# Passage from the output projection to the FFN up projection: first up operand and weights in the last output block, y a block ahead, written order

## Chip, cores and metric

One NeuronCore of a Trainium2 chip. The metric is the device time of one execution in microseconds, given as the median of several runs.

## What is computed

One layer of a hybrid decoder trunk on x (2048 x 1024, float32): a mixer of three head groups (mLSTM, forgetting attention, spatial gating), whose concatenated outputs y are projected back, and a convolutional FFN. The part that matters here:

```python
y = jnp.concatenate([y_attn, y_mlstm, y_sgu], axis=-1)        # (2048, 1024)
x = x + gt1 * (y @ w_out)                                     # output projection, residual
h = rms_norm(x, g_ffn) * (1.0 + sc2) + sh2
z = causal_depthwise_conv(h @ w_up, w_conv, b_conv)           # w_up: 1024 x 5632, width 3
a, gv = jnp.split(z, 2, axis=-1)
x = x + gt2 * ((silu(a) * gv) @ w_down)                       # w_down: 2816 x 1024
```

## The kernel before

It runs as stages: input projection with mLSTM and gating, attention, output projection, up with conv and gate, down. A float32 product is made of three matmuls of split operands (`mm3`, lines 54 to 56: high x high, high x low, low x high). A split is a copy of the high half on ScalarE (ACT) and a subtraction for the low half on VectorE (DVE).

**Output projection** (lines 1237 to 1264). The 2048 rows are four blocks of 512 in the order `TBS` = (2, 3, 0, 1). A block has eight parts `mm(i, nb)`: 128 rows i by a 512-column half nb of w_out, each 8 slices k of the contraction times three matmuls into one of four PSUM banks `wps`. Blocks 0 and 3 (counted in the order of the run) go by halves, the others by rows. `load_split` loads a piece of y or w_out into a buffer `ld` (for the four attention slices two pieces, added), and splits it into `yhl0`/`yhl1` (y; a block and a half fit) or `wo0`/`wo1`. `load_w(1)`, the second half of w_out, is called in block 0; `load_y` for a block at the block's start. `evict` multiplies a bank by the gate, adds x, lets ACT square and sum it, and stores x to DRAM; `stats` and `scale` make the RMS norm (the power is taken on GpSimd, POOL). `turns` transposes a finished block on TensorE (PE), 8 slices of four 128 x 128 transposes into four PSUM tiles `tps`, and ACT moves each slice with scale and shift into `hT`, the operand of up. The blocks of the second half of the sequence (H = 1) are combined and sent to DRAM (`put_d`, through `todo`).

**Up** (lines 1288 to 1404, loop from 1637). The product runs as seven steps p of a Strassen-like scheme for each group g of 128 + 128 columns and each half H. A step is 12 matmuls. Step p uses operand `OF[p]` of the sequence side: B11 and B21 are the first block's halves of hT as they are, B12 and B22 the second's, and T1 = B12 - B11, T2 = B22 - T1, T3 = B22 - B12, T4 = B21 - T2. `b_first` makes one, as 4 split tiles. `prep` makes the weight side (for p 5 and 6 the sums S1, S2 of weight blocks, lines 1326 and 1327), split into `wsp`; `mm` multiplies; `post` reads the PSUM bank on ACT or DVE (s1 for p = 1, u2 for p = 6, line 1366, za for p = 2, zg for p = 7 and 4); p = 2, 7 and 3 add into a bank that p = 1, 6 and 5 began and that s1, u2 and zg read in between. The first two groups run interleaved, step by step: 14 opening steps 0 to 13. `prep` runs three steps ahead (`AHEAD`).

What sets the order: a scheduler lays out each engine's queue from a simulated run, taking the instruction that is ready and stands first in the code. Memory is a stack from each side (`pool.open`, `pool.close`): a tile waits for the earlier tiles at its place. In the kernel before, `w` and B11 lie over buffers of `wo_r2`: `w` mostly over `yhl1`, B11 over `wo1`.

Of the kernel before, what the change touches and what calls it, by code (L numbers as in the profile page):

```python
# [33 lines left out]
def trunk(  # L34
# [257 lines left out]
    def wout_open_right():  # L292
        pool.open("wo_r", "right", ("yhl0", 2048, 16), ("ld", 2048, 3), ("wo0", 2048, 16))
# [845 lines left out]
    def load_y(n, tb):  # L1139

        tag = lambda k: "yhl%d" % ((n * 8 + k) % 12 >= 8)
        part = lambda d, k: d[k * P : (k + 1) * P, tb * TB : (tb + 1) * TB]
        return [load_split(part(yt_d, k), tag(k), V, part(y2_d, k) if k < 4 else None) for k in range(KT)]
# [6 lines left out]
    def put(n, q, t, by_dram=False):  # L1150

        if n == "T2":
            src = t[:, 1, :].bitcast(F32) if by_dram else pool.tile([P, 512], F32, name="t2")
            V.tensor_tensor(src, h_part("B22", q), h_part("T1", q), op=ALU.subtract)
            V.tensor_tensor(h_part("T4", q), h_part("B21", q), src, op=ALU.subtract)
        else:
            src = h_part(n, q)
            if n == "T1":
                V.tensor_tensor(src, h_part("B12", q), h_part("B11", q), op=ALU.subtract)
            elif n == "T3":  # L1160
                V.tensor_tensor(src, h_part("B22", q), h_part("B12", q), op=ALU.subtract)
        A.copy(t[:, 0, :], src)
        V.tensor_tensor(t[:, 1, :], src, t[:, 0, :].bitcast(F32), op=ALU.subtract)

    def put_d(n, q):
        t = pool.tile([P, 2, 512], F32R, name="hl", tag="hl")
        put(n, q, t, True)
        dma(hc_d[COMBO.index(n), q], t.bitcast(F32))

    class Block:  # L1170
        def __init__(self, n, tb):
            self.n, self.tb, self.H, self.half = n, tb, tb // 2, tb % 2
            self.x, self.st, self.ps, self.xn = {}, {}, {}, {}

        def start(self):
            self.y = load_y(self.n, self.tb)
# [45 lines left out]
        def turns(self):  # L1222
            if self.half == 0:
                for k in range(KT):
                    self.turn(k)
                if self.H == 1:
                    for q in range(4):
                        todo.append(lambda q=q: (put_d("B11", q), put_d("B21", q)))
            else:
                for q in range(4):  # L1230
                    self.turn(q)
                    self.turn(4 + q)
                    if self.H == 1:
# [6 lines left out]
    for n, tb in enumerate(TBS):  # L1240
        blk = Block(n, tb)
        blk.start()
        parts = by_nb if n in (0, 3) else by_i
        for j, (i, nb) in enumerate(parts):
            if (n, j) == (0, 4):
                load_w(1)
            blk.mm(i, nb)
            if n == 3 and j > 4:
                continue
# [5 lines left out]
            if j == 1 and before:  # L1255
                before.turns()
# [6 lines left out]
    while todo:  # L1263
        todo.pop(0)()
    pool.close("wo_r2")
# [4 lines left out]
    w_first = [w_load(0), w_load(1)]  # L1270
    hb = {}

    def b_first(n, qs=range(4)):
        for q in qs:
            t = b_tile(n, q)
            hb.setdefault((0, n), []).append(t)
            put(n, q, t)

    blk.evict(0, 1)
    b_first("B11", (0, 1))  # L1280
    blk.stats(0)
    blk.scale(0)
    blk.evict(1, 1)
    b_first("B11", (2, 3))
    blk.stats(1)
    blk.scale(1)
# [10 lines left out]
    def up_open_left():  # L1297
        pool.open(
            "up_l", "left", ("s", 2048, 4), ("sw", 2048, 4), ("T1", 4096, 4), ("B22", 4096, 4), ("t2", 2048, 1), ("hal", 352, 1)
# [6 lines left out]
    class Group:  # L1306
# [12 lines left out]
        def prep(self, p):  # L1319
# [302 lines left out]
    for i in range(AHEAD):  # L1622
        up_groups(-1)
    prep(0)
    blk.evict(2, 1)
    blk.stats(2)
    prep(1)
    blk.scale(2, True)
    blk.evict(3, 1)
# [94 lines left out]
```

## Time and profile before

| | us |
|---|---|
| median of 3 runs | 2631.01 |
| lowest, highest | 2628.65, 2633.12 |
| profiled execution, its own time | 2633.32 |
| its span | 2631.3 |
| PE busy | 2539.3 (97%) |
| DVE busy | 2007.0 (76%) |
| ACT busy | 1269.2 (48%) |
| POOL busy | 398.9 (15%) |

The output projection lies at about 1144 to 1343 us of the span, up from 1347 to 2207, down behind it. Busy shares are means over stages with different limits; a busy PE is not one at its peak, and the granted clock tells how fast it ran.

### The profile page before, as it was taken

The numbers are of one execution on the slowest core, as the hardware profiler recorded it, in microseconds if no ns is written. First come the engines' busy times: TensorE is split into PE (matmuls) and PEld (weight loads), VectorE is DVE, ScalarE is ACT, GpSimd is POOL, SyncE is SP. The second block draws the span as 40 slices with busy tenths as digits, with TensorE's granted clock in tenths as the row PEclk, the third lists the DMA queues.
The fourth block names the chain that finished last, engine by engine and source line by source line (L and its number), as shares of the span: only waits on it lengthen the run. The fifth ranks groups of instructions, "written<-read, shape, count | busy, mean of one in ns | idle before, by whom it ended". The sixth has DMA issues, their size and how long they took to land.

```text
span 2631.3 us, 36459 instructions
## 1 busy us (share of the span) xinstructions
PE 2539.3 (97%) x12537; PEld 2103.0 (80%) x12537; DVE 2007.0 (76%) x3440; ACT 1269.2 (48%) x2420; POOL 398.9 (15%) x532
## 2 busy tenths in 40 slices
PE   5998999989999999999989999999999999999999
PEld 4886888878787887777868888888888888888787
DVE  7577743565368888866769888888888887898797
ACT  4333343333268888853555444544444444444443
POOL 2012210122336665630000000000000000000000
PEclk9999999999999999999999999999999999999999
DMA  7744653334564355247723222246222226648523
GB/s 244 227 135 131 195 163 107 109 88 121 164 176 116 106 146 149 78 153 238 275 76 104 81 88 80 89 145 232 88 88 81 80 72 247 237 162 302 185 96 116
DMA packets 302592, 379.58 MB, mean 144 GB/s; under 512 B 31934, under 2 KB 194588, under 8 KB 300360
## 3 DMA queue, kind: packets, MB, share of 16 engines
q1 hardware_dynamic: 302408, 377.26, 44.7%
q8 instruction: 99, 1.62, 0.2%
q14 instruction: 85, 0.70, 0.1%
HBM read 276.44 MB, written 100.74 MB: 143 GB/s over the span
## 4 chain that ended last, share of the span: by engine, by line
PE 79%; DVE 11%; DMA 4%; issue 2%; ACT 2%; POOL 1%; SPq 0%; DVEq 0%; ACTq 0%; POOLq 0%
PE ub L56 10%; PE ub L54 10%; PE ub L55 10%; PE acc L54 6%; PE acc L56 6%; PE acc L55 6%; PE db L55 4%; PE db L56 4%; PE db L54 4%; PE sp L206 4%; PE tp L259 3%; PE op L245 2%; PE op L246 2%; DVE wspl L1468 2%; PE wps L56 2%
## 5 line engine op out<-in xcount | busy, mean ns | idle before, releaser
L54 PE MATMUL acc<-wh,hh 128*128 128x512 f32 (+2 forms) x768 | 289.2, 378 | 8.5 <-DVE ev L688 6.6
L54 PE MATMUL ub<-T,wsph 128*128 128x512 f32 x704 | 274.2, 390 | 5.8 <-ACT wsph L1336 5.8
L56 PE MATMUL acc<-wh,hl 128*128 128x512 f32 (+2 forms) x768 | 277.3, 364 | 0.3 <-DVE hl L563 0.3
L55 PE MATMUL acc<-wl,hh 128*128 128x512 f32 (+2 forms) x768 | 277.2, 363 | 0.0
L56 PE MATMUL ub<-T,wspl 128*128 128x512 f32 x704 | 273.7, 389 | 1.7 <-DVE wspl L1337 1.7
L55 PE MATMUL ub<-T,wsph 128*128 128x512 f32 x704 | 273.9, 389 | 0.0
L55 PE MATMUL db<-wspl,wsph 128*128 128x512 f32 x616 | 240.3, 390 | 2.0 <-DVE wspl L1468 1.9
L56 PE MATMUL db<-wsph,wspl 128*128 128x512 f32 x616 | 239.6, 389 | 0.0
L54 PE MATMUL db<-wsph 128*128 128x512 f32 x616 | 238.3, 389 | 0.3 <-ACT wsph L1467 0.3
L1336 ACT CAST wsph<-S 128x512 fp32r<-128x512 f32 x176 | 109.7, 623 | 227.2 <-PE ub L55 157.4
L263 DVE TENSOR_TENSOR plo<-tp,phi 128x512 fp32r<-128x512 f32 (+1 forms) x320 | 186.9, 607 | 31.3 <-ACT phi L262 29.1
L54 PE MATMUL ub<-B,wsph 128*128 128x512 f32 x528 | 207.4, 393 | 2.8 <-ACT wsph L1336 2.8
L56 PE MATMUL ub<-B,wspl 128*128 128x512 f32 x528 | 206.9, 392 | 0.3 <-DVE wspl L1337 0.3
L55 PE MATMUL ub<-B,wsph 128*128 128x512 f32 x528 | 207.0, 392 | 0.0
L223 ACT ACTIVATE L<-L,nm 128x1024 f32<-128x1024 f32 (+2 forms) x192 | 172.6, 902 | 36.0 <-DVE nm L212 34.6
L262 ACT CAST phi<-tp 128x512 fp32r<-128x512 f32 (+1 forms) x320 | 160.0, 521 | 41.1 <-PE tp L259 39.5
L259 PE MATMUL tp<-ident,L 128*128 128x128 f32 x1088 | 177.2, 275 | 2.7 <-POOL L L228 0.9
L206 PE MATMUL sp<-kk,q 128*128 128x512 f32 (+3 forms) x640 | 170.0, 377 | 3.3 <-DVE nm L212 2.2
L54 PEld LDWEIGHTS acc<-wh,hh 128*128 128x128 f32 x768 | 148.3, 193 | 27.9 <-DVE ev L688 6.9
L228 POOL TENSOR_SCALAR L<-L,rs 128x1024 f32<-128x1024 f32 (+2 forms) x192 | 167.3, 881 | 11.0
L1467 ACT CAST wsph<-act 128x512 fp32r<-128x512 f32 x132 | 82.2, 623 | 179.3 <-PE db L55 162.5
L56 PEld LDWEIGHTS acc<-wh,hl 128*128 128x128 f32 x768 | 147.2, 193 | 23.0 <-DVE hl L563 0.8
(340 smaller groups left out, 5934.0 us busy)
## 6 DMA issues: line engine op xcount, KB each, us to landing
w<-in_w_up_dram SPq DMA_DIRECT2D x88, 512.0 KB
wd<-in_w_down_dram SPq DMA_DIRECT2D x176, 256.0 KB
wa<-in_w_ada_dram SPq DMA_DIRECT2D x96, 256.0 KB
act_d<-yc SPq DMA_DIRECT2D x44, 512.0 KB
act<-act_d SPq DMA_DIRECT2D x44, 512.0 KB
wr<-in_w_in_dram SPq DMA_DIRECT2D x64, 256.0 KB
q<-q_d SPq DMA_DIRECT2D x128, 128.0 KB
hc_d<-hl SPq DMA_DIRECT2D x28, 512.0 KB
```

What stands on the lines that cost most here:

```text
L54: T.matmul(ps, lh, rh, start=start, stop=False, skip_group_check=resume)
L55: T.matmul(ps, lh, rl, start=False, stop=False, skip_group_check=resume)
L56: T.matmul(ps, ll, rh, start=False, stop=stop, skip_group_check=resume)
L206: T.matmul(sp[:, b : b + bw], q2[n][:, qs], kk[:, s0 + b : s0 + b + bw], start=n == 0, stop=n == 1 and not last)
L223: A.activation(L[c], L[c], AF.Exp, bias=nm[:, n - 1 : n], scale=-1.0, accum_out=rs[:, c : c + 1])
L228: G.tensor_scalar(t, t, rs[:, 0:1], 1.0, op0=ALU.mult, op1=ALU.mult)
L245: T.matmul(op[:, c0:], vv[:, j, :], hi[:, c0:], start=(j == 0), stop=False)
L259: T.transpose(tp[:, i * P : (i + 1) * P], rows[i][j // 8][:, (j % 8) * P : (j % 8 + 1) * P], ident)
L262: A.copy(hi[:, c0:], tp[:, c0:])
L263: V.tensor_tensor(lo[:, c0:], tp[:, c0:], hi[:, c0:].bitcast(F32), op=ALU.subtract)
L1336: A.copy(hi, src)
L1467: A.copy(hi, v)
```

## The change

- Memory: `ld` gets a fourth buffer; `wo_r2` holds `wo1` below `yhl1`, so that in the pool that comes after, B11 lies over `yhl1` and B21 over half of `yhl0`; `w` moves into the pool "zy", which is open during the whole output projection; s1 of the first two groups gets tiles of its own (`s0`), and T2's differences lie in the four tiles `s`.
- `load_y` for block n + 1 is called in block n, two slices at a time.
- A block's transposes come in two halves, behind the second and the third part of the next block; the pushes of H = 1 follow the second half.
- `w_first` is loaded behind the first part of the last block.
- From the end of the output projection to step 15 of up, PE, DVE and ACT run in the written order (`manual_schedule`); POOL and the DMA queue stay with the scheduler. In that order B11 and the weight splits of steps 0 and 1 stand ahead of the last block's evictions; the last transposes stand behind steps 1 and 2; T1's differences follow the first half of them, T2's the second, and T3's and T4's come with their operands.
- S1 and S2 of the first two groups are made on POOL instead of DVE.

The diff, cut:

```diff
     def wout_open_right():
-        pool.open("wo_r", "right", ("yhl0", 2048, 16), ("ld", 2048, 3), ("wo0", 2048, 16))
+        pool.open("wo_r", "right", ("yhl0", 2048, 16), ("ld", 2048, 4), ("wo0", 2048, 16))
...
-        pool.open("up_r2", "right", ("w", 4096, 4), ("B11", 4096, 4), ("B21", 4096, 4), ("T2", 4096, 4))
+        pool.open("up_r2", "right", ("T2", 4096, 4), ("s0", 2048, 2), ("B11", 4096, 4), ("B21", 4096, 4), ("pad", 384, 1))
...
-    pool.open("zy", "left", ("zy", 4104, 8))
+    pool.open("zy", "left", ("zy", 4104, 8), ("w", 4096, 4))
...
-    pool.open("wo_r2", "right", ("ldx", 2048, 1), ("yhl1", 2048, 8), ("wo1", 2048, 16))
+    pool.open("wo_r2", "right", ("wo1", 2048, 16), ("yhl1", 2048, 8))
...
-    def load_y(n, tb):
+    def load_y(n, ks):
+        tb = TBS[n]
...
+    def combine(n, q, src=None):
         if n == "T2":
-            src = t[:, 1, :].bitcast(F32) if by_dram else pool.tile([P, 512], F32, name="t2")
             V.tensor_tensor(src, h_part("B22", q), h_part("T1", q), op=ALU.subtract)
-            V.tensor_tensor(h_part("T4", q), h_part("B21", q), src, op=ALU.subtract)
...
+    def combine_t4(q, t2):
+        V.tensor_tensor(h_part("T4", q), h_part("B21", q), t2, op=ALU.subtract)
...
-        def turns(self):
...
+        def turns(self, part):
+            for q in range(4):
+                self.turn(4 * part + q)
...
+    blks = [Block(n, tb) for n, tb in enumerate(TBS)]
+    blks[0].y += load_y(0, range(KT))
+    for n, blk in enumerate(blks):
...
             blk.mm(i, nb)
+            if n < 3 and (n > 0 and j in (0, 1, 2, 3) or n == 0 and j in (2, 3, 6, 7)):
+                q = (0, 1, 2, 3, 0, 0, 2, 3)[j] if n else {2: 0, 3: 1, 6: 2, 7: 3}[j]
+                blks[n + 1].y += load_y(n + 1, (2 * q, 2 * q + 1))
...
-            if j == 1 and before:
-                before.turns()
+            if j in (1, 2) and before:
+                before.turns(j - 1)
+            if (n, j) == (3, 0):
+                w_first = [w_load(0), w_load(1)]
...
+    in_order = tc.manual_schedule(engines={mybir.EngineType.PE, mybir.EngineType.DVE, mybir.EngineType.Activation})
+    in_order.__enter__()
...
-    w_first = [w_load(0), w_load(1)]
...
+        if n == "T1":
+            for q in qs:
+                t2.append(combine("T2", q, pool.tile([P, 512], F32, name="t2", tag="s")))
+        elif n == "T3":
+            for q in qs:
+                combine("T3", q)
...
+        if n == "T2":
+            for q in qs:
+                combine_t4(q, t2[q])
...
-    blk.evict(0, 1)
-    b_first("B11", (0, 1))
...
-                V.tensor_tensor(self.S1, A_[2, 1], A_[2, 2], op=ALU.add)
-                V.tensor_tensor(self.S2, self.S1, A_[1, 1], op=ALU.subtract)
+                eng = G if self.H == 0 and self.g < 2 else V
+                eng.tensor_tensor(self.S1, A_[2, 1], A_[2, 2], op=ALU.add)
+                eng.tensor_tensor(self.S2, self.S1, A_[1, 1], op=ALU.subtract)
...
-                self.s1 = self.tmp("s1", "s")
+                self.s1 = self.tmp("s1", "s0" if H == 0 and g < 2 else "s")
...
+    b_first("B11")
     prep(0)
...
     prep(1)
...
+    for i in range(4):
+        blk.evict(i, 1)
+        if i:
+            blk.scale(i - 1, i > 2)
+        blk.stats(i)
     b_first("B21", (0, 1))
-    blk.stats(3)
-    b_first("B21", (2,))
     blk.scale(3, True)
-    b_first("B21", (3,))
+    b_first("B21", (2, 3))
     prep(2)
...
         if i == 1:
-            blk.turns()
+            for q in steps[:2]:
+                groups[q[1], q[2]].post(q[3])
+            blk.turns(0)
+            for q in range(4):
+                combine("T1", q)
+        if i == 2:
+            groups[s[1], s[2]].mm(s[3])
+            blk.turns(1)
...
+        if i == 16:
+            in_order.__exit__(None, None, None)
...
-        prep(i + AHEAD)
-        up_groups(i + AHEAD)
-        if i != n_open and i != 1:
+        if i == 0 or i >= 16:
+            prep(i + AHEAD)
+            up_groups(i + AHEAD)
+        if i not in (1, 2, n_open):
...
+        if i == 2:
+            prep(4)
+        if 2 <= i < 16:
+            prep(i + AHEAD)
+            up_groups(i + AHEAD)
```

## Rows read from the trace of the kernel before

**Rows 1.** Page, part 4: shares of the span in the chain that ended last.

```profile
PE 79%; DVE 11%; DMA 4%; issue 2%; ACT 2%; POOL 1%; SPq 0%; DVEq 0%; ACTq 0%; POOLq 0%
```

**Rows 2.** Busy us by stretches: length, PE, PEld, DVE, ACT, POOL, PEclk, DMA share, GB/s.

```profile
1330.00:1340.00 10.00, 10.00 (x46) 8.29 (x45) 4.86 (x10) 1.45 (x4) 0.55 (x1) 1.00 0.18 72
1340.00:1350.00 10.00, 6.93 (x31) 5.17 (x30) 7.63 (x15) 6.95 (x14) 1.27 (x2) 0.84 1.12 302
1350.00:1360.00 10.00, 9.17 (x40) 6.71 (x38) 5.28 (x10) 3.74 (x6) 0.11 (x1) 0.82 0.00 0
1360.00:1370.00 10.00, 5.65 (x19) 4.47 (x20) 10.00 (x18) 10.00 (x20) 0.00 (x0) 0.83 0.01 2
...
1476.00:1495.00 19.00, 19.00 (x85) 15.74 (x84) 15.98 (x21) 9.29 (x17) 0.00 (x0) 1.00 0.26 84
```

**Rows 3.** PE's timeline, passage: start, duration, line, operands, idle time before and releaser.

```profile
1342.44 0.39 PE L56 MATMUL wps<-wo1h,yhl0l 128*128 128x512 f32 x1
...
1346.95 0.79 PE L54 MATMUL ub<-B,wsph 128*128 128x512 f32 x1 [2.81 <-ACT wsph L1336]
...
1364.35 0.79 PE L54 MATMUL ub<-T,wsph 128*128 128x512 f32 x1 [4.59 <-ACT wsph L1336]
...
1384.73 0.50 PE L56 MATMUL ub<-T,wspl 128*128 128x512 f32 x1 [1.72 <-DVE wspl L1337]
...
1395.10 0.39 PE L54 MATMUL ub<-B,wsph 128*128 128x512 f32 x1
...
1400.54 0.39 PE L54 MATMUL ub<-B,wsph 128*128 128x512 f32 x1
```

**Rows 4.** PE's timeline in the output projection, blocks 1 and 2.

```profile
1201.38 0.50 PE L54 MATMUL wps<-wo0h,yhl0h 128*128 128x512 f32 x1 [0.59 <-ACT yhl0h L131]
...
1203.46 0.40 PE L54 MATMUL wps<-wo1h,yhl1h 128*128 128x512 f32 x1
...
1208.92 1.91 PE L1217 MATMUL tps<-ident,x 128*128 128x128 f32 x16
1211.95 0.66 PE L1217 MATMUL tps<-ident,x 128*128 128x128 f32 x4 [1.13 <-ACT hz L1218]
...
1214.69 0.39 PE L54 MATMUL wps<-wo0h,yhl1h 128*128 128x512 f32 x1
...
1257.56 1.91 PE L1217 MATMUL tps<-ident,x 128*128 128x128 f32 x16
...
1263.01 0.39 PE L54 MATMUL wps<-wo0h,yhl0h 128*128 128x512 f32 x1
```

**Rows 5.** DVE's timeline around the last transposes.

```profile
1357.07 0.69 DVE L1159 TENSOR_TENSOR hz<-hz 128x512 f32<-128x512 f32 x1 [4.37 <-ACT hz L1218]
...
1360.52 0.68 DVE L1326 TENSOR_TENSOR S<-w 128x512 f32<-128x512 f32 x1
```

**Rows 6.** Timelines of POOL and DVE, output projection.

```profile
1169.80 1.29 POOL L132 TENSOR_TENSOR wo1l<-ld,wo1h 128x512 fp32r<-128x512 f32 x1 [10.19 <-ACT wo1h L131]
1175.71 1.29 POOL L132 TENSOR_TENSOR wo1l<-ld,wo1h 128x512 fp32r<-128x512 f32 x1 [4.62 <-ACT wo1h L131]
...
1170.35 1.29 DVE L1196 TENSOR_TENSOR x<-x,yg 128x512 f32<-128x512 f32 x1
...
1175.77 1.78 DVE L1196 TENSOR_TENSOR x<-x,yg 128x512 f32<-128x512 f32 x1
...
1338.15 0.69 DVE L1196 TENSOR_TENSOR x<-x,yg 128x512 f32<-128x512 f32 x1
```

**Rows 7.** DMA queue's timeline, and w_out's second half: shortest/median/longest ns, first and last start.

```profile
1172.27 0.81 SPq L297 DMA_DIRECT2D ld<-in_w_out_dram  x2
...
L54 PE MATMUL wps<-wo1h,yhl0h x96: 389/389/389, 1174.8 to 1342.0; 128*128 128x512 f32 x96
```

**Rows 8.** DVE's and ACT's timelines: runs of like instructions, back to back.

```profile
1386.40 2.48 DVE L1163 TENSOR_TENSOR B<-hz,B 128x512 fp32r<-128x512 f32 x4
...
1342.64 3.74 ACT L1162 CAST B<-hz 128x512 fp32r<-128x512 f32 x7 [2.98 <-PE wps L55]
```

More of the change, by code (lines that the diff above doesn't have):

```diff
@@ L1137, in trunk @@
     todo = []
-    def load_y(n, tb):
+    def load_y(n, ks):
+        tb = TBS[n]
         tag = lambda k: "yhl%d" % ((n * 8 + k) % 12 >= 8)
         part = lambda d, k: d[k * P : (k + 1) * P, tb * TB : (tb + 1) * TB]
-        return [load_split(part(yt_d, k), tag(k), V, part(y2_d, k) if k < 4 else None) for k in range(KT)]
+        return [load_split(part(yt_d, k), tag(k), V, part(y2_d, k) if k < 4 else None) for k in ks]
     def h_part(n, q):
@@ L1148, in h_part, with halves_of, put @@
         return hT[i + q][:, j * 512 : (j + 1) * 512]
-    def put(n, q, t, by_dram=False):
+    def combine(n, q, src=None):
         if n == "T2":
-            src = t[:, 1, :].bitcast(F32) if by_dram else pool.tile([P, 512], F32, name="t2")
             V.tensor_tensor(src, h_part("B22", q), h_part("T1", q), op=ALU.subtract)
-            V.tensor_tensor(h_part("T4", q), h_part("B21", q), src, op=ALU.subtract)
[L1156 to L1161, printed above, removed]
+            return src
+        src = h_part(n, q)
+        if n == "T1":
+            V.tensor_tensor(src, h_part("B12", q), h_part("B11", q), op=ALU.subtract)
+        elif n == "T3":
+            V.tensor_tensor(src, h_part("B22", q), h_part("B12", q), op=ALU.subtract)
+        return src
+    def combine_t4(q, t2):
+        V.tensor_tensor(h_part("T4", q), h_part("B21", q), t2, op=ALU.subtract)
+    def halves_of(src, t):
         A.copy(t[:, 0, :], src)
         V.tensor_tensor(t[:, 1, :], src, t[:, 0, :].bitcast(F32), op=ALU.subtract)
+    def put(n, q, t):
+        src = combine(n, q, t[:, 1, :].bitcast(F32))
+        if n == "T2":
+            combine_t4(q, src)
+        halves_of(src, t)
     def put_d(n, q):
         t = pool.tile([P, 2, 512], F32R, name="hl", tag="hl")
-        put(n, q, t, True)
+        put(n, q, t)
         dma(hc_d[COMBO.index(n), q], t.bitcast(F32))
@@ L1172, in __init__ @@
             self.n, self.tb, self.H, self.half = n, tb, tb // 2, tb % 2
-            self.x, self.st, self.ps, self.xn = {}, {}, {}, {}
-        def start(self):
-            self.y = load_y(self.n, self.tb)
+            self.x, self.st, self.ps, self.xn, self.y = {}, {}, {}, {}, []
         def rows(self, i):
@@ L1220, in turn @@
             )
-        def turns(self):
[L1223 to L1227, printed above, removed]
-                        todo.append(lambda q=q: (put_d("B11", q), put_d("B21", q)))
[L1229 to L1233, printed above, removed]
+        def turns(self, part):
+            for q in range(4):
+                self.turn(4 * part + q)
+            if self.H == 1 and part == 1:
+                for q in range(4):
+                    if self.half == 0:
+                        todo.append(lambda q=q: (put_d("B11", q), put_d("B21", q)))
+                    else:
                         todo.append(lambda q=q: (put_d("T1", q), put_d("T3", q)))
@@ L1276, in b_first @@
             hb.setdefault((0, n), []).append(t)
-            put(n, q, t)
-    blk.evict(0, 1)
-    b_first("B11", (0, 1))
[L1281 to L1286, printed above, removed]
+            halves_of(t2[q] if n == "T2" else h_part(n, q), t)
+        if n == "T2":
+            for q in qs:
+                combine_t4(q, t2[q])
     pp.open("up_r", "right", ("ub0", 2048, 4))
@@ L1298, in up_open_left @@
         pool.open(
-            "up_l", "left", ("s", 2048, 4), ("sw", 2048, 4), ("T1", 4096, 4), ("B22", 4096, 4), ("t2", 2048, 1), ("hal", 352, 1)
+            "up_l", "left", ("s", 2048, 4), ("sw", 2048, 4), ("T1", 4096, 4), ("B22", 4096, 4), ("hal", 352, 1)
         )
@@ L1653, in trunk @@
         if i == 1:
-            blk.turns()
+            for q in steps[:2]:
+                groups[q[1], q[2]].post(q[3])
+            blk.turns(0)
+            for q in range(4):
+                combine("T1", q)
+        if i == 2:
+            groups[s[1], s[2]].mm(s[3])
+            blk.turns(1)
             pool.close("wo_l")
```

14 lines of the change are left out of this document (6 added, 8 removed).

## Prediction

> **What bounds the kernel now.** I read the chain of work that ended last first: TensorE (PE) carries 79% of it, VectorE (DVE) 11% [rows 1]. So time is lost where PE is not fed, and I looked for such places from the output projection to the third group of up, the only part that the diff touches.
>
> The passage. The busy time in stretches of 10 us shows PE at 6.93, 9.17 and 5.65 of 10 between 1340 and 1370, with a granted clock of 0.84, 0.82 and 0.83 (about a third of each stretch at 1.2 instead of 2.4 GHz), while DVE goes from 4.86 before it to 10.00 [rows 2]. PE's own timeline gives the sum [rows 3]. Two whole steps (24 matmuls) take 1400.54 - 1395.10 = 5.44 us, so a matmul takes 0.227 and a step 2.72. The last output matmul starts at 1342.44 and is through at 1342.67; the first step of the third group starts at 1400.54: 57.9 us. In between lie 14 steps (38.1 us) and 32 transposes (16 take 1.91 us [rows 4], so 3.8): 41.9 us. **16.0 us are lost.** Idle gaps of 2.81, 4.59 and 1.72 us make 9.1 of it, and the low clock after the first two most of the rest. The first gap waits for the first up weights, cast late; the second for DVE's differences after the transposes; the third for DVE.
>
> The output stage. PE's timeline shows three smaller holes [rows 4]. At the start of the second block the last pieces of y are late: 0.59 us idle, then 2.08 us (1201.38 to 1203.46) for six matmuls that need 1.36, so 1.3 us. Then all 32 transposes of a block come at once: from 1208.92 to 1214.69 they and three matmuls take 5.77 us against 3.82 + 0.68, with 1.13 us of waiting for ACT to empty the PSUM tiles; from 1257.56 to 1263.01 it is 5.45. That is 1.3 and 0.95 us. Together 3.5 us.
>
> **The change part by part.**
> *Transposes in two halves* (turns(0), turns(1), a step apart): four PSUM tiles take four passes without waiting, so the 2.2 us go. ACT has 5.4 us, a matmul step, to empty four tiles, which takes it half of that time. The pushes to DRAM start one step later in block 3 of 4; they end in the last block, where nothing waits for them.
>
> *y a block ahead, a fourth `ld` buffer*: y's late pieces are in `ld` before the old ones are dead; the 1.3 us go. But the loads of the second block's y, eight of its twelve, now stand in SP's queue and in the `ld` rotation ahead of the second half of w_out. Before, the last two of those loads were issued at 1172.27, the first of the two was subtracted on POOL from 1175.71 to 1177.0; PE started on this half at 1174.8 and came to that slice, the seventh, six times 0.68 us later, at 1178.9 [rows 6, 7]: 1.9 us of slack. Cost from 0 (four buffers rotate now, and seven of the eight loads read what attention wrote long before) to two more turns of the rotation, as eight loads in four buffers are: 2 x 4.7 (1172.27 to 1177.0) less the slack, 7.5 us. It is nearer to zero, since those loads can go out while attention ends, before PE needs them; I take 0.8. The stage gains 3.5 - 0.8 = **2.7 us**.
>
> *First weights, first operand*: `w` gets its own place in the pool "zy" and is loaded at the start of the last block, eight steps of 5.44 us before its use; B11 lies over `yhl1`, dead after the third block, and `wsp` over w_out's first half. So the eight halves of B11 and the first two weight splits fall into the end of the output stage, where DVE is busy 4.86 of 10 us [rows 2]; steps 0 and 1 follow the last output matmul at once, and the first gap (2.81 us) and its low clock go. The four loads (2 MB) meet y, x and the DRAM pushes near 1300; x is wanted only when a tile's matmuls are through, so I cost that at nothing. If that cover fails, the last block's eviction and with it a PSUM bank come late.
>
> *Written order on PE, DVE and ACT.* I laid the three queues out by hand from the end of the last output matmul (time 0), each instruction at its row's price: DVE 0.60 us apiece (four take 2.48, of which the last lasts 0.68), ACT casts 0.52 (seven in 3.74) [rows 8]. DVE: last eviction, two scales, statistics, B21, two weight splits, to 7.4. T1's four differences follow ACT's copies of the passes to 10.2. T2's four come next in the order and wait for passes 4 to 7: 11.3 to 14.0. Then 24 instructions without a hole (halves of T1, two splits, halves of T2, T4's differences, two splits, T3's differences and halves): 28.4. Two weight differences each with a cast on ACT and a split behind it, 2.0 apiece, as DVE must wait for the cast in its order: 32.4. Only then does u2 read step 6's bank: 33.1. PE: steps 0 to 7 and the transposes need 25.6 and, with 2.6 us of waiting for T1 and T2, end at 28.2; step 8 adds into the bank that u2 reads, so PE stands 4.9 us. The other six steps take 16.3 and a wait of 0.9 for the second u2. In the third group the copy s1 stands on ACT behind the halo copies of the second, which DVE's backlog holds; after step 16 the order is free again and other steps fill part of that: 1.6. Sum of PE's losses 2.6 + 4.9 + 0.9 + 1.6 = 10.0, 6.0 less than before. A gap of 4.59 us was followed by the low clock before, so the one of 4.9 may be: 0 to 1.7 us (half of some 3.4). I take 0, as PE waits for DVE again right behind it.
>
> *S1, S2 of the first two groups on POOL*: four DVE instructions less (2.4 us, in the 10.0 already), but not for nothing. POOL needs 1.29 us for such a one, and a DVE instruction with both operands in SBUF that ran beside it took 1.29 and 1.78 us, where the same line takes 0.69 alone [rows 6]: 0.60 and 1.09 more, 0.85 in the mean. Does it fall into the passage? Before, DVE stood idle for 4.37 us to 1357.07, though the weights were there (step 0 ran with them at 1346.95 [rows 3]), and did S only at 1360.52, behind the transposes [rows 5]: its tile lies in a pool that opens after them. POOL's order then has S behind the last tile's rsqrt, at some 4 us, where DVE is full. So from 0 (run before the end of the output) to 4 x 1.29 = 5.2; I take 4 x 0.85 = 3.4, the mean of the two rows. The passage gains 6.0 - 3.4 = **2.6 us**.
>
> The Trainium skill ("SBUF — State Buffer", section "Who interferes with whom") says that a DVE instruction with two SBUF inputs and a GpSimd one that reads SBUF exclude each other for the whole instruction. The two rows agree in kind; by that rule the price would be the upper bound, 5.2 us, and the sum 2627.5; the rival of the full lock is this case.
>
> Sum: 2.7 + 2.6 = 5.3 us. The profiled execution took 2633.3 us in a span of 2631.3; less 5.3 it is 2628.0. It is 2.3 us above the median of the three runs, 2631.0, so the forecast there is **2625.7 us**, a fall of 0.2%, which is also about what a measurement of this kernel can tell from no change.
>
> **The rivals.**
> *Faster: S does not collide.* POOL does S during the last output block, when DVE is idle half of the time. Then the passage gains 6.0 and, with no cost at w_out, the stage 3.5: 2621.5. For it: POOL has nothing else to do there. Against: rows 5.
> *Full lock, full chain.* Each of the four POOL instructions holds DVE for its 1.29 us, and the clock falls in the 4.9 us gap with half of its 1.7 us left uncovered: the passage gains 6.0 - 5.2 - 0.8 = 0; the stage 2.7 less 1 for a late w_out: 2629.3. For it: DVE has no idle time from 1360 to 1400 in which to catch up. Against: the start of the passage has 1.2 us of waiting that takes some of it.
> *Slower: DVE hands its backlog on.* The place is the end of the written order, the third group (steps 14 to 18), where conv's and the gate's instructions stand ahead of the splits. With the full lock the losses are 15.2; the 4.4 us that s1 holds step 16 back are not filled (2.9 more), and the clock falls in two gaps (1.7 each). DVE is busy for 16.0 of a group's 19 us later on [rows 2], so a backlog of 8 us lasts for nearly three groups, and where the splits, u2 and zg keep to the order, PE waits some 2 us in each. Losses of 15.2 + 2.9 + 3.4 + 6 = 27.5, 11.5 more than before; the stage still gains 2.7: 2640. Against it: in the kernel before DVE was as full at 1400 and PE waited no more. It decides at step 16: if PE starts it over 3 us after step 15, this is the case.
> *The change doesn't do what it says*: w or B11 is not ready at time 0, because w's loads stand behind x and the DRAM pushes in SP's queue. Then the first gap of 2.8 us stays with its clock (another 3): the passage loses 3 where I have a gain of 2.6, the stage keeps its 2.7: 2631.
>
> **How the numbers follow.** Forecast 0.40 (own range 2623 to 2628.5, from 0.5 to 3.5 us at S and 0 to 2 at w_out); no collision 0.24; full lock 0.17; not ready 0.07; slower 0.12. Faster by over 0.2% (under 2625.7): half of the forecast, 0.20, and 0.24, with a little of the full lock: 0.45. Slower by over 0.2%, over 2636.3: 0.12. The rest, 0.43, is within. The range leaves out the slower case and a tail below the fastest: 2619 to 2633.
>
> **What would show it.** Right: the output stage without the gaps of [rows 4], its last matmul some 2 to 3 us earlier; the first up matmul 0.3 us behind it at full clock; then PE idle once for 4 to 6 us before T3's first step with DVE full and u2 as releaser; DVE subtractions of 1.2 to 1.8 us beside POOL's S in the first 12 us of the passage; from the last output matmul to the third group 53 to 56 us. Wrong: S before the end of the output; PE waiting near 1177 for w_out's second half; the first matmul of up waiting for w; any loss after 1450, where nothing should differ. The forecast falls with the S term above all: it is as large as the passage's net gain.

## The result and the profile after

The changed kernel takes **2641.28 us** (median of 6 runs, 2638.43 to 2641.98), the kernel before, beside it, 2629.74 (6 runs, 2627.07 to 2633.12): ratio 1.0038 [1.0027, 1.0048], **11.5 us slower**. The forecast was 2625.7 in a range of 2619 to 2633. The profiled execution took 2641.43 us in a span of 2639.1.

First the passage, where I expected the change to act. Busy time by stretches of the changed kernel, with the columns of [rows 2]:

```profile
1335.00:1345.00 10.00, 8.39 (x44) 6.59 (x42) 9.13 (x11) 7.49 (x14) 6.60 (x5) 1.00 0.13 52
1345.00:1355.00 10.00, 8.60 (x38) 6.89 (x38) 7.70 (x13) 4.14 (x7) 0.72 (x1) 0.83 0.01 2
1355.00:1365.00 10.00, 8.03 (x33) 5.99 (x34) 10.00 (x17) 5.23 (x11) 0.00 (x0) 1.00 0.00 0
1365.00:1375.00 10.00, 5.18 (x20) 3.95 (x19) 8.50 (x15) 6.12 (x12) 0.00 (x0) 0.92 0.00 1
1375.00:1385.00 10.00, 10.00 (x41) 8.11 (x40) 8.71 (x15) 4.36 (x12) 0.00 (x0) 0.90 0.48 138
...
1395.00:1405.00 10.00, 6.25 (x22) 4.58 (x21) 8.30 (x11) 4.60 (x10) 0.00 (x0) 0.83 0.01 3
```

PE's timeline of the changed kernel, which answers to [rows 3]:

```profile
1335.02 0.40 PE L56 MATMUL wps<-wo1h,yhl0l 128*128 128x512 f32 x1
1335.25 0.40 PE L54 MATMUL ub<-B,wsph 128*128 128x512 f32 x1
...
1346.32 0.80 PE L56 MATMUL ub<-B,wspl 128*128 128x512 f32 x1 [2.92 <-DVE wspl L1354]
...
1373.67 0.77 PE L54 MATMUL ub<-T,wsph 128*128 128x512 f32 x1 [4.82 <-DVE u L1383]
...
1391.63 0.40 PE L54 MATMUL ub<-B,wsph 128*128 128x512 f32 x1
...
1394.42 0.40 PE L54 MATMUL ub<-T,wsph 128*128 128x512 f32 x1
...
1401.14 0.80 PE L54 MATMUL ub<-T,wsph 128*128 128x512 f32 x1 [3.75 <-ACT wsph L1353]
1401.73 0.69 PE L54 MATMUL ub<-B,wsph 128*128 128x512 f32 x1
```

The first up matmul starts 0.23 us behind the last output matmul, where [rows 3] has 2.81 us of idle time. But a gap of 2.92 comes at step 2, the 4.82 at step 8, and 3.75 in the third group, where a single matmul of step 17 (1401.14) comes ahead of step 16 (1401.73). Behind each of the three the granted clock falls: 0.83 from 1345, 0.92 and 0.90 on the two sides of 1375, 0.83 from 1395. And then what I had not looked for. In up, from 1450 on, PE is as busy and its clock as full as before, and it does less. Busy time of the kernel before (first fence) and the changed one (second), same columns:

```profile
1450.00:1800.00 350.00, 350.00 (x1546) 289.82 (x1545) 291.15 (x384) 169.07 (x292) 0.00 (x0) 1.00 0.34 117
1800.00:2150.00 350.00, 348.81 (x1539) 288.28 (x1538) 294.41 (x388) 165.10 (x257) 0.00 (x0) 1.00 0.29 92
```

```profile
1450.00:1800.00 350.00, 350.00 (x1525) 285.97 (x1524) 287.87 (x378) 167.16 (x290) 0.00 (x0) 1.00 0.34 115
1800.00:2150.00 350.00, 348.81 (x1519) 284.59 (x1518) 292.17 (x385) 161.43 (x253) 0.00 (x0) 1.00 0.28 91
```

41 matmuls fewer in 700 us, at 0.2267 us each 9.3 us. No wait, no lower clock: each matmul is slower. Which ones, the first matmul of each step tells; PE's timeline of the kernel before, the first three steps B11, B22, T2 of one group (a group runs in the order B11, B22 of the group before it, T2, B21, T1, T3, T4):

```profile
1626.30 0.39 PE L54 MATMUL ub<-B,wsph 128*128 128x512 f32 x1
...
1629.02 0.39 PE L54 MATMUL ub<-B,wsph 128*128 128x512 f32 x1
...
1631.74 0.39 PE L54 MATMUL ub<-T,wsph 128*128 128x512 f32 x1
```

The same of the changed kernel, T4 and then B11, B22, T2, B21, T1, T3:

```profile
1603.85 0.39 PE L54 MATMUL ub<-T,wsph 128*128 128x512 f32 x1
...
1606.57 0.40 PE L54 MATMUL ub<-B,wsph 128*128 128x512 f32 x1
...
1609.36 0.39 PE L54 MATMUL ub<-B,wsph 128*128 128x512 f32 x1
...
1612.10 0.40 PE L54 MATMUL ub<-T,wsph 128*128 128x512 f32 x1
...
1614.89 0.40 PE L54 MATMUL ub<-B,wsph 128*128 128x512 f32 x1
...
1617.69 0.39 PE L54 MATMUL ub<-T,wsph 128*128 128x512 f32 x1
...
1620.42 0.39 PE L54 MATMUL ub<-T,wsph 128*128 128x512 f32 x1
```

Before, a step takes 2.72 us, whichever operand it streams. After, T4 takes 2.72, B11 2.79, B22 2.74, T2 2.79, B21 2.80, T1 2.73. The three slow steps stream the three operands that lie in the pool `up_r2`, whose tiles the change shifts by `("pad", 384, 1)`. The small excess of B22 and T1 lies in their first three matmuls, behind a slow step.

**The account by stages.** From six points of PE's timeline (first and last matmul of the output projection, first matmul of steps 14 and 18 of up, first of down, end of the span) I made this table for all profiled executions; it is what the experiments below are read by. The "passage" starts with the last output matmul.

| kernel | to output proj. | output proj. | passage to step 14 | steps 14 to 17 | up from step 18 | down |
|---|---|---|---|---|---|---|
| before | 1143.91 | 198.53 | 58.10 | 10.88 | 787.73 | 432.15 |
| k1_before_pad384 | 1139.13 | 199.33 | 57.32 | 11.13 | 798.14 | 432.84 |
| k2_before_three_pads | 1141.31 | 199.76 | 57.32 | 11.05 | 794.82 | 432.56 |
| k3_before_all_right_384 | 1143.91 | 200.26 | 57.43 | 10.97 | 794.80 | 431.81 |
| k11_before_pads_32_64_192 | 1142.34 | 199.61 | 56.60 | 11.11 | 799.37 | 434.09 |
| k12_before_pads_96_160_224 | 1142.52 | 199.28 | 58.03 | 11.19 | 800.45 | 432.59 |
| k10_before_stage_only | 1139.08 | 196.38 | 57.21 | 10.88 | 787.70 | 431.40 |
| changed | 1138.64 | 196.37 | 56.61 | 16.57 | 798.14 | 432.77 |
| k4_after_in_step | 1138.81 | 196.95 | 56.43 | 16.52 | 787.68 | 433.99 |
| k5_in_step_S_on_dve | 1140.21 | 196.36 | 55.43 | 16.83 | 787.70 | 433.43 |
| k7_in_step_order_to_28 | 1140.40 | 196.41 | 56.55 | 15.60 | 794.43 | 432.71 |
| k6_in_step_free_order | 1139.76 | 196.62 | 53.01 | 10.88 | 787.71 | 432.97 |
| k8_free_order_S_on_dve | 1140.62 | 195.85 | 54.15 | 10.88 | 787.76 | 433.23 |
| k9_after_free_order | 1140.34 | 196.69 | 52.98 | 11.13 | 798.14 | 432.96 |

The first column differs by some 5 us between executions of the same code (before, k1 to k3, k11 and k12 run the same up to there), so a stage is compared with its own column, not one span with another.

### The profile page after: what moved, and what is told of

Same layout as the page of the kernel before. It is cut to its first block, busy times and chain, and to the rows that moved or that the text cites. A ratio compares the mean times of both kernels' runs of the same rounds, so it can differ in the third digit from the quotient of the medians.

```text
span 2639.1 us, 36473 instructions
## 1 busy us (share of the span) xinstructions
PE 2547.0 (97%) x12537; PEld 2102.4 (80%) x12537; DVE 2011.0 (76%) x3436; ACT 1268.3 (48%) x2420; POOL 407.7 (15%) x536
## 4 chain that ended last, share of the span: by engine, by line
PE 79%; DVE 10%; DMA 4%; ACT 3%; issue 2%; POOL 2%; SPq 0%; DVEq 0%; ACTq 0%; POOLq 0%
PE ub L54 10%; PE ub L56 10%; PE ub L55 10%; PE acc L54 6%; PE acc L56 6%; PE acc L55 5%; PE db L55 4%; PE db L56 4%; PE sp L206 4%; PE db L54 4%; PE tp L259 3%; PE wps L55 2%; PE wps L56 2%; PE wps L54 2%; PE op L245 2%
```

## Experiments: why up is slower

`wsp`, the weights' tiles, lie in `up_r1` at the right end. The tiles of `up_r1` and `up_r2` are multiples of 2048 bytes, and by the sizes of all pools every operand of up, T1 and B22 in the left pool too, lies a multiple of 512 bytes from the weights in the kernel before ("in step" below). With the pad, B11, B21 and T2 lie 384 bytes off. **My theory:** the distance of the streamed operand from the weights sets the matmul's rate. **The rivals:** a backlog on DVE from the passage; the new neighbours of the tiles.

**k1: the pad alone, in the kernel before.**

```diff
-        pool.open("up_r2", "right", ("w", 4096, 4), ("B11", 4096, 4), ("B21", 4096, 4), ("T2", 4096, 4))
+        pool.open("up_r2", "right", ("w", 4096, 4), ("B11", 4096, 4), ("B21", 4096, 4), ("T2", 4096, 4), ("pad", 384, 1))
```

> The kernel before with one edit: a tile of 384 bytes behind T2 in the pool up_r2, which nobody uses. It moves B11, B21, T2 and w down by 384 bytes, as the change does with B11, B21 and T2; order of work, waits and number of instructions stay. Theory A (the place of the moving operand in SBUF slows the matmul): in the trace of the changed kernel a matmul that streams B11, B21 or T2 starts 0.2332 us after the one before, one that streams T3 or T4 0.2267, and the first three of the step behind such a step 0.232. Per group of up that is 36 x 6.5 ns + 6 x 5 ns = 0.26 us, 11.6 us in 44 groups: about 11 us slower than before, ratio 1.004, all of it between the third group and the end of up; the passage and the output stage as before. Theory B (the loss in up comes from what the change does in the passage: a backlog on VectorE, S on POOL, the written order): no change, within 2 us of before, every up matmul at 0.2267. Theory C (it comes from the new neighbours: w moved to the left pool, so its loads and the splits that read it lie elsewhere): no change either.

Measured: 2642.84 us against 2632.28, ratio 1.0040 [1.0026, 1.0054]; up from step 18 takes 798.14 us, to the hundredth what it takes in the changed kernel. 384 unused bytes cost 10.4 us. The rivals are out: the passage, POOL's work, the order and the pool of `w` are here those of the kernel before.

**k4: the changed kernel with its operands in step.**

```diff
-        ... ("ld", 2048, 4), ("wo0", 2048, 16))
+        ... ("ld", 2048, 4), ("wo0", 2048, 16), ("wpad", 128, 1))
-        ... ("B21", 4096, 4), ("pad", 384, 1))
+        ... ("B21", 4096, 4), ("pad", 512, 1))
```

> The changed kernel with 128 unused bytes at the right end of wo_r and 512 in place of 384 at the right end of up_r2: B11 still lies exactly over yhl1, and all operands of the output projection and of up are now a multiple of 512 bytes from each other. Nothing else differs. Theory A: up runs at 0.2267 throughout, some 10 to 11 us faster than the changed kernel, 2630 to 2631 us, level with before (ratio 0.998 to 1.002); the output stage and the passage stay as in the changed kernel, with the gap of 4.8 us at step 8 and of 3.75 at step 16. Theories B and C: as slow as the changed kernel, ratio 1.004.

Measured: 2630.51 us against 2632.28, ratio 0.9997 [0.9988, 1.0006]; up from step 18 takes 787.68, the passage and the third group are as in the changed kernel. So about 11 us of the changed kernel's time are this distance, and all else that the change does comes out at nothing.

**k3, k2, k11, k12: which distance.** k3 moves the weights along with the operands of the right side and leaves T1 and B22 (left pool) where they are.

```diff
-        ... ("wsp", 2048, 12))
+        ... ("wsp", 2048, 12), ("pad", 384, 1))
```

> The kernel before with the unused 384 bytes at the right end of up_r1: now the weights' tiles wsp, T3, T4, T2, B21 and B11 all move down by 384 bytes, and T1 and B22, in the left pool, stay. If what counts is the place of the moving operand against that of the weights: the five that moved along are fast (0.2267) and T1 and B22, which did not move, are slow (0.233): 24 matmuls of 84 a group, about 7 to 8 us slower in up. If the place of the moving operand alone counts: the five are slow and T1 and B22 fast: some 17 us slower. The down stage reads both its operands from wsp and moves with it: no change there by the first reading, 1848 slower matmuls (some 12 us) by the second. If theory A is wrong: no change.

PE's timeline of k3, again B11, B22, T2, B21, T1, T3:

```profile
1610.15 0.39 PE L54 MATMUL ub<-B,wsph 128*128 128x512 f32 x1
...
1612.88 0.40 PE L54 MATMUL ub<-B,wsph 128*128 128x512 f32 x1
...
1615.67 0.39 PE L54 MATMUL ub<-T,wsph 128*128 128x512 f32 x1
...
1618.40 0.39 PE L54 MATMUL ub<-B,wsph 128*128 128x512 f32 x1
...
1621.12 0.40 PE L54 MATMUL ub<-T,wsph 128*128 128x512 f32 x1
...
1623.91 0.39 PE L54 MATMUL ub<-T,wsph 128*128 128x512 f32 x1
```

Now B11 and B21, slow in k1 at the same addresses, are fast (2.73 and 2.72), and B22 and T1, which have not moved, are slow (2.79 each). So it is not the place of the streamed operand but **its distance from the weights**. Down, whose operands both moved, takes no longer (431.81). k2, k11 and k12 set other distances with small unused tiles.

> The kernel before with three unused tiles of 128 bytes in up_r2, so that T2 moves down by 128, B21 by 256 and B11 by 384 bytes. The weights' tiles wsp stay. It tells which offsets are slow. If any offset from the weights' place within 512 bytes slows a matmul: all three at 0.233, some 10 us slower. If the place within 256 bytes counts: T2 and B21 differ, B21 (256) at 0.2267, T2 (128) and B11 (384) at 0.233, some 7 us slower. If 128 bytes were enough to be in step, nothing would be slower, which the changed kernel (384) already speaks against. If theory A is wrong: all at 0.2267.

> The kernel before with unused tiles of 32, 32 and 128 bytes in up_r2: T2 moves down by 32 bytes, B21 by 64 and B11 by 192; the weights' tiles stay. So far a distance between streamed operand and weights of 256 bytes was fast (0.2267 us a matmul) and one of 128 or 384 slow (0.2326 to 0.2333). If every distance that is not a multiple of 256 is slow: all three at 0.2326 or more. If the cost grows with the distance from the next multiple of 256: T2 at 0.228, B21 and B11 at 0.230. If 128 alone is slow: all three at 0.2267.

> The same with unused tiles of 96, 64 and 64 bytes: T2 moves down by 96 bytes, B21 by 160, B11 by 224. If every distance that is not a multiple of 256 is slow: all three at 0.2326 or more. If the cost grows with the distance from the next multiple of 256: B11 at 0.228, T2 and B21 (96 bytes off on either side) at 0.231. If 128 alone is slow: all three at 0.2267.

From the step starts of 34 groups I took the mean length of a slow step and of the step in step behind it, less 2 x 2.72 us (for two slow steps in a row with one behind them, half of the excess over 3 x 2.72):

| distance, bytes | operand and kernel | excess, us per step |
|---|---|---|
| 32, 64 | T2, B21 in k11 | 0.095 each |
| 96, 160 | T2, B21 in k12 | 0.095 each |
| 128 | T2 in k2 | 0.084 |
| 192 | B11 in k11 | 0.099 |
| 224 | B11 in k12 | 0.125 |
| 256 | B21 in k2 | 0.00 (part of the 0.084 above lies in it) |
| 384 | B11 in k1; T1, B22 in k3 | 0.095; 0.088, 0.091 |
| multiple of 512 | all in before | 0 |

Of the readings put down before, "every distance that is not a multiple of 256 is slow" holds; the cost doesn't grow with the distance. It is 3 to 4.6% of a step of 2.72 us, with what is left to the step behind; the slow step alone takes 2.76 to 2.81 us, 1.6 to 3.2% more. How far it reaches into the step behind, whose operand is in step, differs, and that is why the table takes both: three matmuls of some 0.232 us behind 128 and 384 bytes, six or seven slow ones behind 160 and 224 (k12), ten behind 64 and 192 (k11). k2, k3, k11 and k12 are single profiled executions, so only the lengths of their steps and stages are used; T3 and T4 steps that follow one in step take 2.72 us in them too.

The Trainium skill ("TensorE: Matmul & The Clock Gate", section "Step-by-step: what each phase is for") says that TensorE has two independent read ports in SBUF, one for the streamed operand and one for weight loads, and that loading the next weights takes nothing from the running matmul. At distances that are multiples of 256 no row here speaks against it. At others a step costs 3 to 4.6% more, by a quantity that involves both operands, while a weight load takes 188 ns before and after (289.82 us for 1545 of them, 285.97 for 1524, in the fences on 1450 to 1800). What the two share inside, no run here shows.

## Experiments: the passage and the third group

**k6: no written order** (on top of k4, so that up doesn't cover it): `manual_schedule` is taken out, the code order stays.

```diff
-    in_order = tc.manual_schedule(engines={mybir.EngineType.PE, mybir.EngineType.DVE, mybir.EngineType.Activation})
-    in_order.__enter__()
...
-            in_order.__exit__(None, None, None)
```

> k4_after_in_step without the written order: PE, VectorE and ScalarE stand in the planner's order in the passage too. It tells what the written order is worth by itself. In k4 it costs PE 4.91 us at step 8 (u2 stands behind T3's halves on VectorE) and 3.75 us plus slow matmuls at its end (step 16, where the first matmul of a later step stands ahead and waits for a cast). Theory A (these two gaps come from the order): one or both go, the passage to step 18 is 4 to 9 us shorter than in k4's 72.9: 2622 to 2627 us. Rival (VectorE is full to 1400 whatever the order): the gaps come elsewhere, 0 to 2 us either way. Rival (the planner's order is the bad one, as in the kernel before, whose passage to step 18 takes 69.0 with a first gap that k4 doesn't have): no gain or some us more.

Measured: **2621.61 us against 2632.37, ratio 0.9956 [0.9944, 0.9969]**: faster than both kernels, 10.8 us (0.41%) below k4 by the ratios. In the table the passage falls from 56.43 to 53.01 and the third group from 16.52 to 10.88, together 9.1 us. What DVE waits for tells most of it. DVE in the changed kernel, 1335 to 1408 (who waited for whom: us in total, times, longest):

```profile
DVE wspl L1354 <- ACT wsph L1353: 4.1, 6, 0.9
DVE yg L1205 <- PE wps L56: 2.8, 1, 2.8
DVE t L1155 <- ACT hz L1228: 2.3, 1, 2.3
DVE yc L1409 <- ACT yc L1408: 1.7, 3, 0.8
DVE s L1389 <- PE ub L56: 0.5, 1, 0.5
...
```

and in k6 over the same stretch:

```profile
DVE yg L1205 <- PE wps L56: 1.3, 1, 1.3
DVE x L1219 <- POOL st L128: 1.2, 2, 0.8
DVE wspl L1352 <- ACT wsph L1351: 0.4, 1, 0.4
```

With two more waits of 0.2 us, and without the one for the last output matmul (yg), DVE stands for 9.0 us in the changed kernel (8.8 in k4) and for 1.6 in k6, some 7 of the 9.1 us. In the written order a weight difference, its cast on ACT and its split follow each other, so that DVE stands 0.7 us for each cast; the scheduler puts other work between. DVE is the engine that the passage waits for, and the order makes it stand. That the order costs the time is shown by k6; that it does so by these waits is read from the traces.

The last gap is of a like kind, on ACT. ACT's timeline of the changed kernel, in front of the gap at 1401.14:

```profile
1400.28 0.19 ACT L1399 COPY hal<-za 128x2 f32<-128x2 f32 x1 [1.96 <-DVE za L1397]
...
1400.47 0.61 ACT L1353 CAST wsph<-S 128x512 fp32r<-128x512 f32 x1
```

The cast that PE waits for could have run earlier (the last S before it was written by 1396.9), but stands behind two halo copies, which wait for a DVE that is behind with its work.

**k7: the written order twelve steps longer** (on top of k4), to see whether the gap at 1401 is the seam at the order's end.

```diff
-        if i == 16:
+        if i == 28:
             in_order.__exit__(None, None, None)
```

> k4_after_in_step with the written order ending twelve steps later (step 28 instead of 16). In k4 and in the changed kernel PE loses 5.6 us between steps 14 and 18: it stands 3.75 us with a single matmul of T1 (step 17) that was put ahead of step 16, then seven slow ones. Theory A (the seam: behind the end of the written order the planner puts that matmul first, although its cast stands behind two copies that wait for VectorE): with the end moved, the gap at step 16 goes or falls under 2 us, and unless the seam at 28 brings it back the kernel is 3 to 5 us faster than k4: 2626 to 2627.5 us. Rival (VectorE's backlog is handed on): the gap stays at step 16 or comes in the next steps, and the kernel is as fast as k4 or slower.

Measured: 2636.34 us, ratio 1.0013 [1.0004, 1.0022], some 4 us slower than k4. PE's waits in k7, 1335 to 1450:

```profile
PE ub L54 <- DVE u L1383: 4.6, 2, 3.9
PE ub L54 <- DVE zg L1391: 4.1, 1, 4.1
PE ub L56 <- DVE wspl L1354: 3.8, 3, 2.9
PE ub L54 <- ACT s L1380: 3.5, 1, 3.5
```

The gap at step 16 stays, now with the copy s1 as releaser (3.5), and a new one of 4.1 follows for zg, at 1421; up from step 18 takes 6.7 us more than in k4. So it is not the seam; where the order holds, DVE's backlog is handed on to the next group.

**k5 and k8: S1, S2 back on DVE**, with the written order (on k4) and without (on k6).

```diff
-                eng = G if self.H == 0 and self.g < 2 else V
+                eng = V
```

> The changed kernel with its operands in step (k4_after_in_step), and S1, S2 of the first two groups on VectorE instead of POOL. In k4's trace POOL does the four S in the first ten us of the passage, and VectorE's instructions beside them take longer: the scale of x, two halves of B21 and the two first splits together some 4.2 us more than the same lines elsewhere; then PE stands 2.91 us at the first split and its next eight matmuls start 0.43 us apart. Theory A (collision on the path): without POOL the split comes 4.2 us earlier, this gap and its slow matmuls go (4.5 us), and the four S cost VectorE 2.4 us a little later, ahead of the steps that wait for T1 and T2: from the last output matmul to the third group 2 to 3 us less than in k4, 2627.5 to 2628.5 us. Rival (VectorE's sum alone bounds the passage, PE only stands at another place): the gap moves to step 8, where VectorE's u2 is late: 0 to 1.8 us less. Rival (S on POOL gives what was hoped for): 1 to 3 us more than k4.

> k6_in_step_free_order with S1, S2 of the first two groups on VectorE instead of POOL, as in the kernel before. In k6's trace the four S run on POOL from 1344.0 to 1350.4 and five instructions of VectorE beside them take some 4.2 us more than the same lines elsewhere; behind them PE waits six times for casts and splits, 5.4 us together, until 1376. With S on VectorE these 4.2 us go and four S of 0.6 us come, 2.4. Theory A (VectorE's sum bounds the passage): 1 to 2 us less than k6, 2619.5 to 2620.5 us. Rival (as under the written order, where the same edit moved the gaps and changed nothing): within 0.7 us of k6. Rival (S on POOL is worth it, the lock costs less than the work): 1 to 2.5 us more than k6.

Timelines of POOL and DVE in the changed kernel, the collision:

```profile
1339.30 1.38 POOL L1343 TENSOR_TENSOR S<-w 128x512 f32<-128x512 f32 x1
1340.76 1.60 POOL L1344 TENSOR_TENSOR S<-S,w 128x512 f32<-128x512 f32 x1
1342.33 1.71 POOL L1343 TENSOR_TENSOR S<-w 128x512 f32<-128x512 f32 x1
1344.12 1.59 POOL L1344 TENSOR_TENSOR S<-S,w 128x512 f32<-128x512 f32 x1
...
1338.23 1.29 DVE L1169 TENSOR_TENSOR B<-hz,B 128x512 fp32r<-128x512 f32 x2 [0.16 <-ACT B L1168]
...
1341.16 3.44 DVE L1169 TENSOR_TENSOR B<-hz,B 128x512 fp32r<-128x512 f32 x2
1344.52 2.34 DVE L1354 TENSOR_TENSOR wspl<-w,wsph 128x512 fp32r<-128x512 f32 x2
```

The same two halves take 1.29 us alone and 3.44 beside POOL, two splits 2.34 in place of 1.29, and a scale at 1339.44 1.79 in place of 0.75: 4.2 us of DVE's time. The Trainium skill ("SBUF — State Buffer", section "Who interferes with whom") has it that a DVE instruction with two SBUF inputs and a GpSimd one that reads SBUF exclude each other; the rows of the four subtractions agree in kind.

With S on DVE, under the written order: 2630.55 us, ratio 0.9990 [0.9981, 0.9998], against k4's 0.9997; the first gap is gone (2.91 to 0), the gap of 4.9 at step 8 stays, and the waits for casts grow from 5.3 to 7.0: passage and third group together are 0.7 us shorter. In the free order: 0.9961 [0.9948, 0.9973] against 0.9956, and 1.1 us longer by the table. So **4.2 us of collision and 2.4 us of work saved on DVE come to nothing that the times can tell**, either way.

**k9: written order out, operands out of step**, to close the table of two by two.

> The changed kernel, its operands out of step as they are in it, without the written order. With k4 (in step, written order), k6 (in step, free) and the changed kernel it fills a table of two by two. If the two costs are independent, the loss to the operands' places (11 us, in up) and to the written order (9 us, in the passage) add: 2641.3 - 9 = 2632.4 us, level with before, with the up stage at 0.2327 us a matmul for B11, B21, T2 and no gap at steps 8 and 16. If the written order hid or made part of the loss in up: 2630 or less, or 2635 and more.

Measured: 2632.92 us against 2632.89, ratio 1.0000 [0.9991, 1.0008]. Ratios to before:

| | written order | free order |
|---|---|---|
| operands out of step (384) | 1.0038 (changed) | 1.0000 (k9) |
| in step (512) | 0.9997 (k4) | 0.9956 (k6) |

The two costs add: 0.0038 and 0.0041 for the order, 0.0041 and 0.0044 for the distance, some 10 and 11 us.

## Experiment: the output projection's part alone

**k10**: in the kernel before, `load_y` a block ahead, the fourth `ld`, `ldx` left out, and the transposes in halves.

```diff
-        ... ("ld", 2048, 3), ("wo0", 2048, 16))
+        ... ("ld", 2048, 4), ("wo0", 2048, 16))
...
+                blks[n + 1].y += load_y(n + 1, (2 * q, 2 * q + 1))
...
-            if j == 1 and before:
-                before.turns()
+            if j in (1, 2) and before:
+                before.turns(j - 1)
```

> The kernel before with the part of the change that lies in the output projection alone: y's pieces a block ahead, a fourth buffer ld, the transposes in two halves of 16. First weights, B11 over the dead y, S on POOL, the written order and the places of the operands stay out. The prediction's step: the stage gains 3.5 us (late y 1.3, transposes 1.3 and 0.95) less what the second half of w_out, now behind eight loads of y, comes late. In the profiles so far the output projection (first to last of its matmuls) takes 198.5 to 200.3 us in kernels with the old stage and 196.4 to 197.0 with the new one. Theory A (that difference is the stage's, and it reaches the end): 2 to 3.5 us faster than before. Rival (the gain is given back, since the last block's eviction or the first weights end the passage's first gap anyway): within 1 us of before.

Measured: 2625.57 us against 2632.89, ratio 0.9977 [0.9968, 0.9985], 6 us faster, twice what was expected. The stage itself is 196.38 us long (198.5 to 200.3 with the old stage, in the mean 199.5). The rest lies ahead of it, in attention, where w_out's first half is loaded. ACT's timeline and PE's in the kernel before:

```profile
1048.94 0.62 ACT L131 CAST wo0h<-ld 128x512 fp32r<-128x512 f32 x1 [3.14 <-DMA ld<-in_w_out_dram]
...
1052.52 0.50 PE L245 MATMUL op<-phi,vv 128*128 128x512 f32 x1 [1.57 <-ACT yo L250]
```

With three `ld` tiles ACT stands 3.14 us for a piece of w_out, in its queue ahead of attention's own copies; PE stands 1.57 for one of those, and its granted clock from 1040 to 1060 is 0.91. With the fourth tile ACT's wait for `ld` is 0 in k10 (0.2 us in the changed kernel), the clock there 1.00. From the 500th to the 520th score matmul of attention (line 206) the kernels with three tiles take 10.7 to 12.8 us, those with four 9.7 to 9.8; from the 500th to the first matmul of the output projection 95.6 to 97.3 and 92.7 to 93.4, in the mean 3.5 us less. With the stage's 3 that is the 6 us. The fourth tile by itself was not tried, and where the 1.5 us behind the 520th come from stays open.

## Why the prediction was wrong

**The step that failed: "any loss after 1450, where nothing should differ".** I costed the new layout of `up_r2` as an order of tiles and the 384 bytes as nothing. It is 10.4 us in up (k1), of the 11.5 by which the kernel is slower. It was not one of my rivals, and no row of the kernel before could have priced it, since there every operand of up is in step; but the pad was in the diff, and a bound for "a matmul with another layout" was due for the 1584 matmuls that it moves.

**Output stage: gain 2.7 forecast, 3.0 measured** (mean 199.5 of six profiles with the old stage, 196.5 of eight with the new). The holes of [rows 4] are gone; PE's timeline of the changed kernel has the 16 transposes at 1.91 us without a wait:

```profile
1204.85 1.91 PE L1227 MATMUL tps<-ident,x 128*128 128x128 f32 x16
```

w_out's second half came late, which I had named as a sign of being wrong, but at the small end of 0 to 7.5 us (0.8 taken, 1.5 measured):

```profile
1172.86 0.50 PE L55 MATMUL wps<-wo1l,yhl0h 128*128 128x512 f32 x1 [1.05 <-POOL wo1l L132]
...
1177.69 0.50 PE L55 MATMUL wps<-wo1l,yhl0h 128*128 128x512 f32 x1 [0.46 <-POOL wo1l L132]
```

Missed altogether: the fourth `ld` also ends a wait in attention, and the last part of attention takes some 3.5 us less in the kernels that have it. I had read only the stage in whose pool the buffer is used.

**Passage: gain 4.2 to step 14 forecast, 0.9 measured** (16.0 of losses less 2.6, 4.9, 0.9 and 3.4; mean 57.5 of six profiles with the old passage, 56.6 after). The hand-laid queues held: the first matmul 0.23 us behind the last output matmul (0.3 forecast), S on POOL at 4.05 us (4 forecast), a gap of 4.82 with u2 as releaser (4.9 forecast). PE's waits came to 9.8 us (2.92, 4.82 and 2.1 for T1 and T2), less than the 11.8 of the sum: S's price was about right, 3.4 taken and 4.2 measured on DVE, and it made the first gap, 2.92; DVE had u2 done at 38.3 us, not 33.1, but PE came to step 8 late as well, at 33.6 instead of 28.2. The term that failed here is the **clock**, which I set at nothing behind the gap of 4.9 ("I take 0, as PE waits for DVE again right behind it"). PE didn't wait again: it is busy for 10.00 us of the ten from 1375, at a clock of 0.90, and the clock fell behind the first gap too, to 0.83. The last output matmul, the steps and the transposes are 42.1 us without loss, so 56.6 has 14.5 of losses; less the waits, 4.7 us are slow matmuls, some 0.4 of them by the distance (4.3 in k4). Where the sum had 11.8 of waits and no clock, it was 9.8 and 4.7.

**Third group: loss 1.6 forecast, 5.7 measured** (0.25 of it the distance, by k9). I named the mechanism (a copy on ACT behind halo copies that DVE's backlog holds) and wrote that the free order from step 16 fills part of it. It doesn't: from the start of step 15 it is 6.72 us, 4.0 over a step, until PE starts anything else, and that is the one matmul of step 17; step 16 follows 0.6 us later, and the clock is 0.83 from 1395 to 1405.

**The slower rival** was decided at this point ("over 3 us"), and its number, 2640, is nearly the result; that the number fits is luck. It was right only for the place: the backlog on DVE, handed on in the written order, is shown by k6 and k7. Its 6 us of waits in the next groups never came: behind step 18 PE has no such gap. Most of the time went elsewhere, into the distance of the operands.

**S on POOL**: I called it the term on which the forecast stands or falls. In k5 and k8 moving it changes nothing that the times can tell. **Not ready**: excluded by the 0.23 us.

So the parts, by the ratios of the runs: output projection with the fourth `ld` -6 us (k10); first weights, B11 over the dead y, S on POOL and what else k6 has of the change a further -5.5 (k6 against k10, 0.9956 against 0.9977); the written order +10.8 (k4 against k6); the distance +10.8 (changed against k4). Taken from ratio to ratio they add up by construction to the changed kernel's own, 1.0038, which is 10 us; its medians differ by 11.5. Each part has an interval of 2 to 4 us on either side. Down takes 432.7 to 434.0 us with the new layout and 431.4 to 434.1 with the old: no difference that these executions show.

## What to carry to other kernels

When a change moves tiles, compare the time from one matmul to the next in a stage that it doesn't touch, and keep the byte distance between a streamed operand and its weights a multiple of 256. In a written order on the engine that is the bottleneck, look for each instruction that waits for another engine's answer to the one just ahead; put other work between, or leave that engine to the scheduler, which here (k6) gave 0.9956 of the time before. A buffer that feeds a cast is worth looking up on the queue of the engine that casts: what stands behind the cast waits too, in whatever stage that is.

## What the runs showed of the hardware

A float32 matmul of 128 x 512 starts 0.2267 us after the one before if streamed operand and weights lie a multiple of 256 bytes apart in their partitions (256 and multiples of 512 tried), and in the mean of a step 0.230 to 0.234 if they don't (32, 64, 96, 128, 160, 192, 224 and 384 tried). The first three to ten matmuls behind such a step are slower too, though their own operand is in step. A busy share of 100% and a clock of 1.00 show nothing of it, so the granted clock doesn't tell all of how fast PE ran, as the section on the profile before has it; the count of matmuls in a stretch does.
